# Second norm's column sums set one by one between large products, the hand-written order carried through the fourth pair, and other banks and scaling in the last norm

## The chip, the cores and the metric

One NeuronCore of a Trainium2 chip. The metric is the device time of one execution in microseconds (us); the time before is the median of 3 runs, and one further execution was profiled. Engines: PE is TensorE, DVE VectorE, ACT ScalarE, POOL GpSimd, SP SyncE (it issues the DMAs).

## The reference

One decoder layer on x of 1 x 1024 x 1024 in float32, with a final norm (D_MODEL 1024, D_FF 4096, 16 heads of 64, 2 key/value heads, window 128):

```python
def rms_norm(x, g):
    y = xf * lax.rsqrt(jnp.mean(xf * xf, axis=-1, keepdims=True) + RMS_EPS)
    return (y * g.astype(jnp.float32)).astype(x.dtype)

x = x + swa_mixer(rms_norm(x, attn_norm), w_qkv, sinks, w_o)   # sliding window 128, sinks, ALiBi
u = rms_norm(x, mlp_norm) @ w_up
x = x + square(relu(u)) @ w_down                               # 1024 -> 4096 -> 1024
out = rms_norm(x, final_norm)
```

The last lines are put together from the reference's layer; the change touches the second norm, the product with w_up, and the last norm.

## The kernel before

**Layout.** Features lie on the 128 partitions, tokens along the free axis, so h[0] to h[7] hold 128 features x 1024 tokens each. The tokens are cut into two halves (HALVES, 0 to 511 and 512 to 1023). A product in float32 is made of three passes over operands that are split in a high and a low part (names with _h and _l): high x high, high x low, low x high. So a "product of a 128x128 block" is three matmuls of 512 columns. A split is a copy on ScalarE (the high part) and a subtraction on VectorE (the low part).

**Order of work.** Attention comes first; then the second part of the output projection, blocks o_m_hf of 12 matmuls each (oblock, m = 0 to 7, first for half 0, then for half 1); oadd adds a block to h on VectorE, and square puts its square, made on ScalarE, into one of three parts: the running sum sq_0 (m = 0 to 5) and sq_6, sq_7 alone. The second norm of a half takes 4 column sums of each part (a matmul of 128x1 with ones; stat_sum), makes 1/rms from them (rstd, five small VectorE operations n_st and one on ScalarE), a diagonal matrix dg of it, and one matmul that spreads it over the partitions (stat_bcast, n2b). first_half makes x = h * gain * n2b for half 0, second_half for half 1.

**The up product** is made for 16 pairs p of 256 hidden units, each by seven products (numbers 1 to 7) of sums and differences of quarters instead of eight, 12 matmuls each. Weights: wa (for products 1, 2), and from the sums of raw weights s1, s2 (ws, products 5, 6), s3, s4 (wt, 7, 3), and wb (a22, product 4). Inputs: xb (products 1, 2), xt (5, 6), xu (7, 4), xc (3). PSUM tags X, Y and Z hold the sums of a pair; snapshot copies X to oa or ob, and relu2, c11_relu, c11_add and up_evac add, square and store the results.

**Who sets the order.** TensorE runs in the order of the code everywhere. VectorE, ScalarE and GpSimd do so while `e.ordered` is set: from the second half of the output projection through product (6, 2), where (n, p) is product n of pair p. After that a scheduler places their operations. The queue `tiny` holds single small matmuls: each call of mm takes one of them after its own matmul, as the first norm's sums do:

```python
    def mm(out, lhsT, rhs, start, stop, **kw):
        pe.matmul(out, lhsT=lhsT, rhs=rhs, start=start, stop=stop, **kw)
        if tiny:
            tiny.pop(0)()
```

**Slots.** Split weights of later pairs come from a ring of twelve slots over three tags (walloc, ring_up); raw weights wu come by DMA in two loads per pair (up_load, or up_first and up_sums), and four GpSimd operations make their sums sa and sb (in place for pair 2).

**The tail.** Seven down products of the same kind; the last (6) goes in four output blocks mp for each quarter of the tokens, ps_q[q][mp], of 256 columns; mmq issues their matmuls, and VectorE adds each finished block to h. finish is the last norm of a stretch of tokens: sums, diagonal, broadcast n3b, and eight multiplications with gain and n3b, two to an output DMA.

Line 41 of the profile is the helper that emits every operation, so groups are told apart by tile.

Of the kernel before, what the change touches and what calls it, by code (L numbers as in the profile page):

```python
# [62 lines left out]
def trunk(tc, xT, gains, wqkv, wo, wup, wdn, bias_d, sinks_d, ident_d, mask_d, outT):  # L63
# [588 lines left out]
    def square(m, hf):  # L652
# [17 lines left out]
    def his(src, alloc, name):  # L670
# [38 lines left out]
    def b22_split(i):  # L709
        XP["b22", i] = split1(h[2 * i + 1][:, HALVES[1]], atile if i else ktile, f"xc{i}")  # L710
# [153 lines left out]
    for p in range(2):  # L864
        WU["a22", p] = split1(SUM[p][0][:, 1], wtile, f"wb{p}")
# [4 lines left out]
    def oblock(m, hf):  # L870
        ps = bank(obanks[(hf * KT + m) % 5], f"o1_{m}_{hf}")
        for kk in range(4):
            mm3(ps, wsl(ws[m // 2], (m % 2) * 4 + kk), o_t[4 + kk], HALVES[hf], kk == 0, kk == 3)
# [11 lines left out]
    for m in range(KT):  # L885
        ps = oblock(m, 1)
# [6 lines left out]
        if m == 6:  # L893
            WU["s2", 0], WU["s1", 0] = LO["ws0"]()
        oadd(m, 1, ps)
        if m == 0:
            stat_sum(0)
# [14 lines left out]
    WU["s3", 0], WU["s4", 0] = LO["wt0"]()  # L912
    up_mms(1, 0, {2: lambda: stat_sum(1)})
    LO["wa3"] = his(wu3, ktile, "wa3")
# [7 lines left out]
    for p in range(4):  # L922
# [12 lines left out]
        if p == 1:  # L935
            LO["ws1"] = his(SUM[1][1], otile, "ws1")
        second_half(p + 1, rb)
        XP["t2", p], XP["t1", p] = LO[p]()
        up_mms(2, p + 1)
# [36 lines left out]
    c11_relu(0)  # L976
    up_product(6, 2)
    LO["wt1"] = his(SUM[1][2], otile, "wt1")
    WU["s3", 1], WU["s4", 1] = LO["wt1"]()
    c11_relu(1)  # L980
    c11_add(3)
    for e in (v, s, g):
        e.ordered = False
    for i in range(4):
        b22_split(i)
    for p in (2, 3):
        c11_relu(p)
    WU["a22", 2] = split1(u2[1][:, 1], walloc, "wb2")
    WU["s3", 2], WU["s4", 2] = split2(u2[0], walloc, "wt2")
# [198 lines left out]
```

## Time and profile before

| | |
|---|---|
| median of 3 runs | 942.75 us (941.77 to 943.16) |
| profiled execution, its own time | 944.29 us |
| its span | 942.4 us |
| mean granted clock of TensorE | 0.988 |
| PE busy | 918.4 us, 97% |
| DVE busy | 685.3 us, 73% |
| ACT busy | 445.9 us, 47% |
| POOL busy | 291.4 us, 31% |

The span is the time between the first and the last event on the chip; the execution's own time has 1.9 us beside it. The busy shares are means over all stages. A change in one stage is read in the rows of that stage: when an instruction starts, how long it takes, and, in brackets, how long its engine stood idle ahead of it and what ended that.

### The profile page before, as it was taken

What the parts mean: (1) busy time and instruction counts of PE and PEld (TensorE: products, weight loads), DVE (VectorE), ACT (ScalarE), POOL (GpSimd) and SP (SyncE); (2) the same over time, 40 slices, a digit from 0 to 9 for tenths busy, and PEclk for the clock granted to TensorE, in tenths of its full rate; (3) what the DMA queues carried; (4) which work ended last, traced back from release to release, by engine and by line L of the source; (5) the groups of instructions that cost most, each with busy time, mean ns of one, the idle gap of its engine ahead of it and who ended that gap; (6) DMA issues with size and microseconds to landing.
All of it is one profiled execution on the core that took longest, in us unless ns stands there. A gap on an engine that the chain in (4) does not pass through costs nothing.

```text
span 942.4 us, 12606 instructions
## 1 busy us (share of the span) xinstructions
PE 918.4 (97%) x4508; PEld 770.5 (82%) x4508; DVE 685.3 (73%) x956; ACT 445.9 (47%) x846; POOL 291.4 (31%) x254
## 2 busy tenths in 40 slices
PE   8999999999989998999999999999999999999996
PEld 6788888888878776888888888878888888888995
DVE  6789988989738886766675656566968785567964
ACT  8578877877524363433433343334333333445510
POOL 3026656566354015464435543110000000040200
PEclk9999999999989999999999999999999999999998
DMA  8200100510552124544354345789898988347622
GB/s 307 68 29 29 53 29 7 210 43 23 170 160 96 34 89 177 184 165 145 135 173 162 135 142 165 278 281 395 302 359 318 349 299 310 116 157 271 264 90 89
DMA packets 57325, 160.35 MB, mean 170 GB/s; under 512 B 6448, under 2 KB 10288, under 8 KB 57264
## 3 DMA queue, kind: packets, MB, share of 16 engines
q1 hardware_dynamic: 57264, 159.57, 47.7%
q8 instruction: 35, 0.57, 0.3%
q14 instruction: 26, 0.21, 0.1%
HBM read 121.79 MB, written 37.75 MB: 169 GB/s over the span
## 4 chain that ended last, share of the span: by engine, by line
PE 89%; DVE 4%; ACT 3%; issue 1%; POOL 1%; DMA 1%; SPq 0%; DVEq 0%; POOLq 0%; ACTq 0%
PE d L41 33%; PE uX L41 17%; PE f L41 12%; PE uY L41 9%; PE o L41 5%; PE uZ L41 4%; PE pv L41 3%; PE S L41 3%; PE pt L41 1%; PE psv L41 1%; PE psk L41 1%; DMA xr<-xT 1%; PE n2s L41 1%; ACT kh L41 1%; PE n L41 0%
## 5 line engine op out<-in xcount | busy, mean ns | idle before, releaser
L41 PE MATMUL d<-dx_h,dw_h 128*128 128x512 f32 (+1 forms) x512 | 186.5, 364 | 1.0 <-DVE hr L41 1.0
L41 PE MATMUL d<-dx_l,dw_h 128*128 128x512 f32 (+1 forms) x512 | 185.6, 362 | 0.0
L41 PE MATMUL d<-dx_h,dw_l 128*128 128x512 f32 (+1 forms) x512 | 185.6, 362 | 0.0
L41 PEld LDWEIGHTS d<-dx_h,dw_h 128*128 128x128 f32 x512 | 96.6, 189 | 16.8 <-DVE hr L41 1.4
L41 PEld LDWEIGHTS d<-dx_l,dw_h 128*128 128x128 f32 x512 | 96.6, 189 | 15.2 <-issue 0.2
L41 PEld LDWEIGHTS d<-dx_h,dw_l 128*128 128x128 f32 x512 | 96.6, 189 | 14.9
L41 ACT CAST dx_h<-hr 128x1024 fp32r<-128x1024 f32 x56 | 58.5, 1051 | 58.2 <-DVE dx_l L41 23.2
L41 ACT CAST dw_h<-wf 128x1024 fp32r<-128x1024 f32 x40 | 42.0, 1052 | 89.6 <-PE d L41 78.4
L41 DVE TENSOR_TENSOR dx_l<-hr,dx_h 128x1024 fp32r<-128x1024 f32 x56 | 71.6, 1287 | 17.4 <-ACT dx_h L41 16.4
L41 POOL TENSOR_TENSOR ssq3a<-ssq3a,sq_a 128x512 f32<-128x512 f32 x7 | 12.5, 1792 | 208.7 <-ACT sq_a L41 208.3
L41 DVE TENSOR_TENSOR dw_l<-wf,dw_h 128x1024 fp32r<-128x1024 f32 x40 | 48.7, 1220 | 26.0 <-ACT dw_h L41 25.9
L41 POOL TENSOR_TENSOR t<-t,sm 128x512 f32<-128x512 f32 x32 | 33.4, 1042 | 105.1 <-DVE sm L41 105.1
L41 DVE TENSOR_TENSOR wf<-wd,we 128x1024 f32<-128x1024 f32 x40 | 49.6, 1247 | 21.9 <-DMA we<-wdn 10.7
L41 ACT ACTIVATE t<-t,sm 128x129 f32<-128x129 f32 x128 | 50.5, 397 | 10.9 <-DVE sm L41 10.4
L41 PE MATMUL f<-xh,w_h 128*128 128x512 f32 x128 | 53.3, 416 | 0.0
L41 PE MATMUL f<-xl,w_h 128*128 128x512 f32 x128 | 50.4, 394 | 0.0
L41 PE MATMUL f<-xh,w_l 128*128 128x512 f32 x128 | 50.3, 393 | 0.0
L41 PE MATMUL uX<-xu_h,wb 128*128 128x512 f32 x128 | 43.4, 401 | 2.5 <-ACT oa L41 2.5
L41 POOL TENSOR_TENSOR ob<-ob,oa 128x512 f32<-128x512 f32 x16 | 21.6, 1348 | 78.3 <-DVE ob L41 78.3
L41 POOL TENSOR_TENSOR oc<-oc,oa 128x512 f32<-128x512 f32 x16 | 21.0, 1315 | 75.7 <-DVE oc L41 75.7
L41 ACT COPY oa<-uX 128x512 f32<-128x512 f32 x32 | 18.7, 588 | 49.9 <-PE uX L41 49.9
L41 POOL TENSOR_SCALAR_AFFINE_SELECT cur<-hl 128x1024 fp32r<-128x1024 f32 x32 | 39.5, 1235 | 2.0 <-DVE hl L41 2.0
(350 smaller groups left out, 2400.7 us busy)
## 6 DMA issues: line engine op xcount, KB each, us to landing
wd<-wdn SPq DMA_DIRECT2D x56, 512.0 KB, 5.8
hr<-hid SPq DMA_DIRECT2D x56, 512.0 KB, 5.0
we<-wdn SPq DMA_DIRECT2D x40, 512.0 KB, 6.8
hid<-oa SPq DMA_DIRECT2D x32, 256.0 KB, 2.4
hid<-oc SPq DMA_DIRECT2D x32, 256.0 KB, 2.2
hid<-ob SPq DMA_DIRECT2D x32, 256.0 KB, 2.3
w_r<-wqkv SPq DMA_DIRECT2D x8, 512.0 KB, 4.0
h<-xT SPq DMA_DIRECT2D x8, 512.0 KB, 6.4
```

The costliest lines, as they stand in the source:

```text
L41: ins = method(*args, **kw)
```

## The change

It has three parts. First, stat_part queues the second norm's sums in `tiny`, one between two large matmuls; for half 0 in o_0_1 (parts sq_6, sq_7, sq_0), for half 1 the running sum in the second half of o_7_1, sq_6 and sq_7 in product (1, 0). In half 1 the running sum's last addition goes to GpSimd, and some splits and one load move. Second, the hand-written order reaches through pair 3, with the products of pairs 0 to 3 in another order. Third, in the last product neighbouring blocks mp lie in different banks, and the last stretch's norm scales by the gain on ScalarE beforehand, so that three VectorE operations and two output DMAs remain.

```diff
+    def stat_part(hf, i):
+        first, last = (i == 1, i == 0) if hf == 0 else (i == 0, i == 2)
+        if first:
+            stat["ps", hf] = bank("Y", f"n2s{hf}")
+        ps, sq = stat["ps", hf], stat["sq", hf][i]
+        for b in range(4):
+            tiny.append(lambda b=b: pe.matmul(
+                ps[:, b:b + 1], lhsT=sq[:, b * P:(b + 1) * P], rhs=ones[:, 0:1], start=first and b == 0,
+                stop=last and b == 3, skip_group_check=True))
     def stat_sum(hf):
-        ps = bank("Y", f"n2s{hf}")
-        parts = stat.pop(("sq", hf))
-        for i, sq in enumerate(parts):
-            colsum(ps, sq, 4, i == 0, i == len(parts) - 1)
-        rn2 = rstd(ps, 4, f"n2_{hf}")
+        while tiny:
+            tiny.pop(0)()
+        rn2 = rstd(stat["ps", hf], 4, f"n2_{hf}")
...
-            (g if m < 5 else v).tensor_tensor(parts[0], parts[0], sq, op=ALU.add)
+            (v if hf == 0 and m == 5 else g).tensor_tensor(parts[0], parts[0], sq, op=ALU.add)
...
-        return ring(W * 2 + O * 2 + [ktile, atile] + W * 4 + O * 2)
+        return ring(W * 2 + O * 2 + [atile, atile] + W + O * 2 + W * 3)
...
-    for p in range(2):
-        WU["a22", p] = split1(SUM[p][0][:, 1], wtile, f"wb{p}")
...
     for m in range(KT):
-        ps = oblock(m, 1)
+        if m == 0:
+            for i in (1, 2, 0):
+                stat_part(0, i)
+        ps = oblock(m, 1, (lambda: stat_part(1, 0)) if m == 7 else None)
+        if m == 0:
+            stat_sum(0)
         if m == 1:
             rb = stat_bcast(0)
...
+        if m in (3, 4):
+            WU["a22", m - 3] = LO["wb", m - 3]()
         oadd(m, 1, ps)
         if m == 0:
-            stat_sum(0)
...
+        if m in (1, 2):
+            LO["wb", m - 1] = his1(SUM[m - 1][0][:, 1], wtile, f"wb{m - 1}")
...
     s2_2 = up_sums_inplace(2, *u2)
-    up_mms(1, 0, {2: lambda: stat_sum(1)})
+    stat_part(1, 1)
+    stat_part(1, 2)
...
+    up_mms(1, 0)
+    stat_sum(1)
...
     up_product(6, 2)
...
+    up_mms(7, 0)
+    c22_sum(0)
...
+    up_mms(7, 1)
+    c22_sum(1)
+    WU["s3", 2], WU["s4", 2] = LO["wt2"]()
+    s2_3 = up_sums_inplace(3, *u3)
+    up_product(4, 0)
+    up_product(3, 0)
+    d1_sum(1)
+    c11_relu(2)
+    up_product(4, 1)
+    up_mms(5, 2)
+    up_product(3, 1)
+    c11_relu(3)
+    WU["s2", 3] = split1(s2_3, walloc, "ws3a")
...
+    up_product(7, 2)
+    WU["s3", 3], WU["s4", 3] = split2(u3[0], walloc, "wt3")
+    up_product(6, 3)
+    up_product(4, 2)
+    EARLY = 4
+    raw4 = up_first(EARLY, walloc)
+    up_mms(5, 3)
+    up_product(3, 2)
+    up_sums(EARLY, raw4, temp)
+    up_product(7, 3)
     for e in (v, s, g):
         e.ordered = False
...
-    order = [(7, 0), (7, 1), (4, 0), (3, 0), (5, 2), (4, 1), (6, 3), (3, 1), (7, 2), (5, 3), (4, 2), (3, 2),
-             (7, 3), (1, 4), (4, 3), (2, 4), (3, 3)]
+    order = [(4, 3), (2, EARLY), (3, 3)]
...
+        if t1 == T:
+            rb = ps[:, 0:n].unsqueeze(1)
+            for i in range(2):
+                k, hg = 4 - i, hgs[i]
+                v.tensor_tensor(hg[:, 0:k], hg[:, 0:k], rb.to_broadcast([P, k, n]), op=ALU.mult)
+                if i:
+                    v.scalar_tensor_tensor(hg[:, k], h[7][:, sl], gn[:, 2, 7:8], ps[:, 0:n],
+                                           op0=ALU.mult, op1=ALU.mult)
+                nc.sync.dma_start(outT[:, 4 * i:4 * i + 4, sl], hg)
+            return
...
-    ps_q = [[banks[2 * q + mp // 2][:, (mp % 2) * 256:(mp % 2) * 256 + 256] for mp in range(4)] for q in range(2)]
+    ps_q = [[banks[2 * q + mp % 2][:, (mp // 2) * 256:(mp // 2) * 256 + 256] for mp in range(4)] for q in range(2)]
...
+            for m in (2 * mp, 2 * mp + 1) if mp < 2 else (4, 5, 6):
+                s.activation(hgs[m // 4][:, m % 4], h[m][:, 768:1024], AF.Copy, scale=gn[:, 2, m:m + 1])
```

TensorE, from the last block of the output projection's half 0 into block o_0_1 of half 1 (o is the block's PSUM bank, wo a weight, oh and ol the attention's output; n2s holds the column sums). Before:

```order
L41 MATMUL o_0_1_3142<-oh_2741,wo_0_l 128x512
L41 MATMUL n2s_3158<-ones,sq_0_0_3023 128x1 x4
L41 MATMUL n2s_3158<-ones,sq_6_0_3124 128x1 x4
L41 MATMUL n2s_3158<-ones,sq_7_0_3140 128x1 x4
L41 MATMUL o_1_1_3194<-oh_1876,wo_0_h 128x512
```

Now:

```order
L41 MATMUL o_0_1_3137<-oh_1876,wo_0_h 128x512
L41 MATMUL n2s_3136<-ones,sq_6_0_3118 128x1
L41 MATMUL o_0_1_3137<-ol_1877,wo_0_h 128x512
L41 MATMUL n2s_3136<-ones,sq_6_0_3118 128x1
L41 MATMUL o_0_1_3137<-oh_1876,wo_0_l 128x512
L41 MATMUL n2s_3136<-ones,sq_6_0_3118 128x1
```

The twelve sums stood in one block behind o_0_1; now each has a large matmul ahead of it, the first one behind the first matmul of o_0_1. In half 1 the running sum is asked for in o_7_1, now:

```order
L41 MATMUL o_7_1_3334<-oh_2473,wo_3_h 128x512
L41 MATMUL n2s_3341<-ones,sq_0_1_3172 128x1
L41 MATMUL o_7_1_3334<-ol_2474,wo_3_h 128x512
L41 MATMUL n2s_3341<-ones,sq_0_1_3172 128x1
L41 MATMUL o_7_1_3334<-oh_2473,wo_3_l 128x512
```

where before all twelve sums of half 1 stood behind the ninth matmul of product (1, 0).

VectorE, from the norm's small operations of half 0 (n_0_st) to the first x products (wb is the low part of a22 of pairs 0 and 1, dg the diagonal). Before:

```order
L41 TENSOR_TENSOR h_2044<-o_0_1_3142,h_2044 128x512
L41 TENSOR_SCALAR n_0_st<-n2s_3158 128x4
L41 RECIPROCAL n_0_st<-n_0_st 128x4
L41 TENSOR_TENSOR n_0_st<-n_0_st 128x4
L41 SCALAR_TENSOR_TENSOR n_0_st<-n_0_st 128x4
L41 TENSOR_TENSOR wb_3003<-wu0b,wb_3003 128x512
L41 TENSOR_TENSOR wb_3006<-wu1b,wb_3006 128x512
L41 SCALAR_TENSOR_TENSOR n_0_st<-n_0_st 128x4
L41 TENSOR_TENSOR dg_0_3178<-ident,n_0_st 128x512
L41 TENSOR_TENSOR h_2046<-o_1_1_3194,h_2046 128x512
L41 SCALAR_TENSOR_TENSOR x_0_3213<-h_2044,gn,n2b_3207 128x512
```

Now:

```order
L41 TENSOR_TENSOR h_2058<-o_7_0_3120,h_2058 128x512
L41 TENSOR_SCALAR n_0_st<-n2s_3136 128x4
L41 RECIPROCAL n_0_st<-n_0_st 128x4
L41 TENSOR_TENSOR n_0_st<-n_0_st 128x4
L41 SCALAR_TENSOR_TENSOR n_0_st<-n_0_st 128x4 x2
L41 TENSOR_TENSOR dg_0_3169<-ident,n_0_st 128x512
L41 TENSOR_TENSOR h_2044<-o_0_1_3137,h_2044 128x512
L41 TENSOR_TENSOR h_2046<-o_1_1_3184,h_2046 128x512
L41 SCALAR_TENSOR_TENSOR x_0_3203<-h_2044,gn,n2b_3197 128x512
```

The two wb splits no longer stand between the small operations and the diagonal; they stand later, behind the splits of x_1 and x_2. The add of o_0_1 stands behind the diagonal now.

ScalarE, around the copies of product 7 of pairs 0 and 1 (oa from uX; xc, wt, ws and wb are high parts). Before:

```order
L41 CAST wt_h<-wu2c 128x1024
L41 CAST xc_3663<-h_2058 128x512
L41 COPY oa_3400<-uX_3362 128x512
L41 COPY oa_3440<-uX_3427 128x512
L41 CAST ws_h<-sa_3702 128x1024
L41 CAST wb_3712<-wu3b 128x512
```

Now:

```order
L41 CAST xc_3655<-h_2050 128x512
L41 CAST xc_3664<-h_2054 128x512
L41 CAST xc_3666<-h_2058 128x512
L41 COPY oa_3396<-uX_3366 128x512
L41 ACTIVATE oa_3436<-oa_3436 128x512 x2
L41 CAST wt_h<-wu2c 128x1024
L41 COPY oa_3436<-uX_3423 128x512
L41 ACTIVATE oc_3730<-uX_3366 128x512
```

The copy of pair 0 stood behind the wt cast of pair 2, and the ws cast, which reads GpSimd's sums of pair 3, right behind the copies; now the wt cast follows the copy of pair 0, and the two relus of pair 1 stand between.

## Rows read from the trace of the kernel before

**Rows 1.** Page, part 1: busy us, share of the span, instructions.

```profile
PE 918.4 (97%) x4508; PEld 770.5 (82%) x4508; DVE 685.3 (73%) x956; ACT 445.9 (47%) x846; POOL 291.4 (31%) x254
```

**Rows 2.** Windows: busy of PE, PEld, DVE, ACT, POOL; granted clock; DMA share; GB/s.

```profile
260.00:280.00 20.00, 17.81 (x84) 14.67 (x82) 6.56 (x14) 5.85 (x9) 11.54 (x10) 0.91 0.43 140
274.00:276.00 2.00, 2.00 (x6) 1.51 (x6) 0.70 (x4) 0.00 (x0) 0.56 (x1) 0.50 0.20 33
```

**Rows 3.** TensorE's timeline, second norm: start, us, operation, count, [idle before <-releaser].

```profile
267.90 0.39 PE L41 MATMUL o<-oh,wo_h 128*128 128x512 f32 x1
...
270.62 2.73 PE L41 MATMUL n2s<-ones,sq 128*128 128x1 f32 x24
...
280.41 1.83 PE L41 MATMUL n2b<-dg,ones 128*128 128x512 f32 x2 [2.60 <-DVE dg L41]
281.25 1.41 PE L41 MATMUL o<-oh,wo_h 128*128 128x512 f32 x1
...
308.42 1.02 PE L41 MATMUL n2b<-dg,ones 128*128 128x512 f32 x2
```

**Rows 4.** TensorE's timeline, 346 to 377 us, from (7, 1) to (4, 2).

```profile
346.07 0.39 PE L41 MATMUL uX<-xu_h,wt_l 128*128 128x512 f32 x1
348.24 0.50 PE L41 MATMUL uX<-xu_h,wb 128*128 128x512 f32 x1 [1.77 <-ACT oa L41]
...
372.42 0.50 PE L41 MATMUL uY<-xt_h,ws_h 128*128 128x512 f32 x1 [2.13 <-DVE ob L41]
...
376.86 0.40 PE L41 MATMUL uX<-xu_h,wb 128*128 128x512 f32 x1
```

**Rows 5.** TensorE's timeline, first norm's sums between large matmuls.

```profile
30.27 0.28 PE L41 MATMUL n_ps<-ones,ssq 128*128 128x1 f32 x2
...
30.73 0.28 PE L41 MATMUL n_ps<-ones,ssq 128*128 128x1 f32 x2
```

**Rows 6.** Timelines of ACT, DVE and POOL, second norm, picked.

```profile
267.94 0.63 ACT L41 ACTIVATE sq<-h 128x512 f32<-128x512 f32 x1 [3.86 <-DVE h L41]
...
278.26 0.69 DVE L41 TENSOR_TENSOR wb<-wu0b,wb 128x512 fp32r<-128x512 f32 x1 [3.49 <-ACT wb L41]
...
279.67 0.69 DVE L41 TENSOR_TENSOR dg<-ident,n_st 128x512 f32<-128x512 f32 x1
...
282.28 2.72 DVE L41 SCALAR_TENSOR_TENSOR x<-h,gn,n2b 128x512 f32<-128x512 f32 x4 [1.32 <-PE n2b L41]
284.92 1.22 DVE L41 TENSOR_TENSOR xb_l<-x,xb_h 128x1024 fp32r<-128x1024 f32 x1
...
287.97 2.01 DVE L41 TENSOR_TENSOR xb_l<-x,xb_h 128x1024 fp32r<-128x1024 f32 x1
...
295.43 0.68 DVE L41 TENSOR_TENSOR h<-o,h 128x512 f32<-128x512 f32 x1
...
287.61 1.30 POOL L41 TENSOR_TENSOR sq<-sq,sq 128x512 f32<-128x512 f32 x1 [4.57 <-ACT sq L41]
```

**Rows 7.** ScalarE's timeline, copies and casts of the middle.

```profile
347.61 1.06 ACT L41 COPY oa<-uX 128x512 f32<-128x512 f32 x2
...
369.45 1.05 ACT L41 CAST ws_h<-sa 128x1024 fp32r<-128x1024 f32 x1 [6.02 <-POOL sa L41]
```

**Rows 8.** TensorE's timeline, last product, between two blocks.

```profile
911.45 0.28 PE L41 MATMUL d<-dx_h,dw_l 128*128 128x256 f32 x1
912.24 0.39 PE L41 MATMUL d<-dx_h,dw_h 128*128 128x256 f32 x1 [0.52 <-DVE hr L41]
```

**Rows 9.** VectorE's timeline at the end; window (VectorE's busy, clock, DMA share, GB/s).

```profile
935.88 3.22 DVE L41 SCALAR_TENSOR_TENSOR out<-hr,gn,n3b 128x256 f32<-128x256 f32 x8 [0.79 <-PE n3b L41]
...
940.00:940.50 0.50, 0.00 (x0) 0.50 0.98 340
```

**Rows 10.** Timelines of ACT and PE, pair 5: sums' cast, first use.

```profile
392.08 1.06 ACT L41 CAST ws_h<-sa 128x1024 fp32r<-128x1024 f32 x1
...
414.95 0.39 PE L41 MATMUL uX<-xt_h,ws_h 128*128 128x512 f32 x1
```

More of the change, by code (lines that the diff above doesn't have):

```diff
@@ L677, in los, with his1 @@
             return [(hi[:, i], lo[:, i]) for i in range(2)]
+        return los
+    def his1(src, alloc, name):
+        x = two(alloc(F32R, name))
+        s.copy(x[:, 0], src)
+        def los():
+            v.tensor_tensor(x[:, 1], src, x[:, 0].bitcast(F32), op=ALU.subtract)
+            return x[:, 0], x[:, 1]
         return los
@@ L911, in trunk @@
     s2_2 = up_sums_inplace(2, *u2)
-    WU["s3", 0], WU["s4", 0] = LO["wt0"]()
-    up_mms(1, 0, {2: lambda: stat_sum(1)})
-    LO["wa3"] = his(wu3, ktile, "wa3")
+    stat_part(1, 1)
+    stat_part(1, 2)
+    LO["wa3"] = his(wu3, wtile, "wa3")
+    WU["s2", 0], WU["s1", 0] = LO["ws0"]()
+    up_mms(1, 0)
+    stat_sum(1)
     snapshot(1, 0)
@@ L934, in trunk @@
         snapshot(1, p + 1)
-        if p == 1:
+        if p == 0:
+            LO["wt0"] = his(SUM[0][2], otile, "wt0")
+        if p == 2:
             LO["ws1"] = his(SUM[1][1], otile, "ws1")
@@ L938, in trunk @@
         XP["t2", p], XP["t1", p] = LO[p]()
+        if p == 0:
+            WU["s3", 0], WU["s4", 0] = LO["wt0"]()
         up_mms(2, p + 1)
@@ L976, in trunk, with c22_sum, d1_sum @@
     c11_relu(0)
-    up_product(6, 2)
-    LO["wt1"] = his(SUM[1][2], otile, "wt1")
-    WU["s3", 1], WU["s4", 1] = LO["wt1"]()
-    c11_relu(1)
-    c11_add(3)
+    LO["wt1"] = his(SUM[1][2], wtile, "wt1")
+    LO["wb", 2] = his1(u2[1][:, 1], walloc, "wb2")
+    b22_his(0)
+    WU["s3", 1], WU["s4", 1] = LO["wt1"]()
+    WU["a22", 2] = LO["wb", 2]()
+    up_product(6, 2)
+    b22_his(1)
+    b22_lo(0)
+    c11_add(3)
+    u3 = up_load(3)
+    b22_lo(1)
+    b22_his(2)
+    b22_his(3)
+    def c22_sum(p):
+        c22 = OUT["a", p][:, 1]
+        OUT["d", p] = temp(f"od{p}")
+        s.copy(c22, PS["X", p])
+        v.tensor_tensor(c22, PS["Y", p], c22, op=ALU.add)
+        relu2(c22, c22)
+        store(5, p, c22)
+    def d1_sum(p):
+        c11, c22 = OUT["a", p][:, 0], OUT["a", p][:, 1]
+        v.tensor_tensor(OUT["d", p][:, 0], c11, c22, op=ALU.add)
+        store(1, p, OUT["d", p][:, 0])
+    up_mms(7, 0)
+    c22_sum(0)
+    b22_lo(2)
+    b22_lo(3)
+    c11_relu(1)
+    LO["wt2"] = his(u2[0], walloc, "wt2")
+    d1_sum(0)
+    up_mms(7, 1)
[11 more added lines that the diff above has]
+    WU["s2", 3] = split1(s2_3, walloc, "ws3a")
+    WU["s1", 3] = split1(u3[1][:, 0], walloc, "ws3b")
+    WU["a22", 3] = split1(u3[1][:, 1], walloc, "wb3")
+    up_product(7, 2)
[8 more added lines that the diff above has]
+    up_product(7, 3)
     for e in (v, s, g):
         e.ordered = False
[L984 to L989, printed above, removed]
-    EARLY = 4
-    order = [(7, 0), (7, 1), (4, 0), (3, 0), (5, 2), (4, 1), (6, 3), (3, 1), (7, 2), (5, 3), (4, 2), (3, 2),
-             (7, 3), (1, 4), (4, 3), (2, 4), (3, 3)]
+    up_product(1, EARLY)
+    up_splits(EARLY)
+    order = [(4, 3), (2, EARLY), (3, 3)]
     for p in range(EARLY, NG):
@@ L996, in trunk @@
         order += ([(1, nxt)] if nxt < NG else []) + [(4, p)] + ([(2, nxt)] if nxt < NG else []) + [(3, p)]
-    ready = 3
     for n, p in order:
-        if (n, p) == (7, 1) or (n == 6 and p >= EARLY - 1):
-            while ready <= min(max(p + 1, 3), NG - 1):
-                raw = up_first(ready, walloc) if ready >= EARLY else None
-                up_sums(ready, raw, temp)
-                up_splits(ready)
-                ready += 1
+        if n == 6 and p + 1 < NG:
+            up_sums(p + 1, up_first(p + 1, walloc), temp)
+            up_splits(p + 1)
         up_product(n, p)
@@ L1112, in trunk @@
     fa = None
+    hgs = []
     for gg in range(NG // 2):
@@ L1117, in trunk @@
             for mp in range(4):
-                mmq(0, 2 * gg + e, mp, 2 * gg + e == 0 and mp % 2 == 0)
+                mmq(0, 2 * gg + e, mp, 2 * gg + e == 0 and mp < 2)
         if gg < 4:
@@ L1129, in trunk @@
         for g_ in range(NG):
-            mmq(1, g_, mp, g_ == 0 and mp % 2 == 0)
+            mmq(1, g_, mp, g_ == 0 and mp < 2)
             if g_ in (5, 11):
```

19 lines of the change are left out of this document (11 added, 8 removed).

## The prediction, made before the changed kernel was run

> **What bounds the kernel now.** I read the page's busy shares first. TensorE is busy 97% of the span [rows 1], so the time falls only where TensorE waits or runs slowly. The windows come next: the granted clock of the 20 us from 260 is 0.91, and inside it there is a stretch at 0.50, the lower of the two levels, 1.2 rather than 2.4 GHz [rows 2]. Last I read TensorE's timeline through the two places that the change rewrites, the second norm [rows 3] and the hand-over from the hand order to the later pairs [rows 4].
>
> The pace comes from rows 3: twelve large products start between 267.90 and 270.62, 2.72 us, so one takes 0.227 us. The price of one fall of the clock comes from rows 4: after the wait at 372.42, twelve products take until 376.86, 4.44 us, so a fall costs 4.44 − 2.72 = 1.72 us. What went ahead of a fall is in the same rows: the 24 one-column products from 270.62, and idle stretches of 2.60, 1.77 and 2.13 us [rows 3, 4].
>
> **The second norm.** From 267.90 to the second half's broadcast at 308.42, TensorE takes 40.52 us [rows 3]. What it has to do there: 117 large products (12 for each of o_0_1 to o_7_1, 12 of product 1, 9 of product 2), 117 × 0.227 = 26.5; 24 column sums of two passes, 2 × 2.73 = 5.5; one broadcast of two passes, about two large products, 0.45. That is 32.4, and 8.1 are lost: the 2.60 idle, and the rest the slow clock behind the sums and behind the idle.
>
> The change sums the same columns, one between two large products. The first norm does this already: from one sum there to the next is 0.46 us [rows 5], of which 0.227 is the large product, so a spread sum costs 0.23, and 24 cost 5.6. So the spreading by itself saves no TensorE work (0.1 more). It can win only what is lost now, 8.0 at most.
>
> What of it comes back, in order. (1) The first single sum needs sq_6, which ScalarE has at 267.94 + 0.63 = 268.57 [rows 6], while TensorE now wants it after one large product, at 267.90 + 0.23 = 268.13: a new wait of 0.4, with the hand-over 0.5. (2) The sums then end at 268.4 + 5.5 = 273.9, o_1_1 at 276.6. The chain to the diagonal stood behind the two weight splits wb in VectorE's order, which waited 3.49 us [rows 6]; with them gone from there it has 2.7 us of o_1_1 as cover, and its own length is the five small operations and the 0.69 of the diagonal, about 2. So I take no wait here; the broadcast starts at 276.6 and o_2_1 at 277.1, not 281.25. (3) VectorE's x products start when the broadcast has ended (1.02 at full clock [rows 3]), at 277.65 rather than 282.28. From there to the add of o_5_1 at 295.43 VectorE had 13.15 us of work without a gap [rows 6]; the two wb splits now stand in between, 2 × 0.65 more. So that add comes at 292.1, then 0.68 for it, 0.63 for the square on ScalarE, 1.30 for GpSimd's add, which the change has put in VectorE's place, and 0.2 of hand-overs: the running sum is ready at 294.9. (4) TensorE asks for it after the seventh matmul of o_7_1, at 277.1 + 5 × 2.72 + 7 × 0.227 = 292.3. It waits 2.6 there; before, nothing was asked for until o_7_1 and three quarters of product 1 were through. Behind that sum on TensorE's queue stand the rest of o_7_1 and all of product 1, so nothing fills the wait.
>
> How sure is 2.6? One split of x took 2.01 us at 287.97 and its neighbour 1.22, with GpSimd's add from 287.61 for 1.30 beside the long one [rows 6]. Two of the four are long; if the shifted times keep both apart from GpSimd, the wait shrinks by 2 × 0.79 to about 1.1; if the other two are hit as well, it grows to 4.2. I take 2.6, where the order of VectorE and GpSimd against each other stays as it is. The Trainium skill (SBUF — State Buffer, Who interferes with whom) says that a VectorE instruction with two SBUF inputs contends with a GpSimd instruction that reads SBUF, and that the first to issue holds the shared ports for its whole length. The trace agrees as far as it goes: 0.94 of GpSimd's add was left when the long split began, and the split took 0.79 longer. By that rule the add moved to GpSimd would also meet the split of x_3, which makes the wait the upper bound of 4.2, another 1.6 from the gain (the third rival below).
>
> (5) After an idle stretch of 2.6 the clock fell before [rows 3], so I take one fall, 1.72. Gain of this part: 8.0 − 0.5 − 2.6 − 1.7 = **3.2**.
>
> The other moved steps here (loads of u2, splits of wt0, wa3 and ws1) lie on engines with room, and their users are products 3 to 7 and pair 3, tens of microseconds later; I take zero. Without that cover a 1024-wide split is 1.22.
>
> **The middle.** From 346.30 (0.23 behind the last product at 346.07) to 376.86 eight up products of 12 stand on TensorE: 8 × 2.72 = 21.76 of 30.56 us, 8.8 lost [rows 4]: two named waits of 1.77 and 2.13, two falls of 3.44 together, and small waits and restarts. The first wait is for the copy of uX(7,0), which ScalarE began only at 347.61, behind casts and relus; the second is for ob, whose copy stood on ScalarE behind the cast of sa for pair 4, and that cast waited 6.02 us for GpSimd's sums [rows 7]. The hand order removes both causes: the copy of uX(7,0) stands behind three short casts and can start when (7,0) ends, 2.72 ahead of the 346.30 at which (4,0) needs it; the casts of pair 4's sums now stand behind the last copy of pair 3. What could be late next is the low part of ws3a, which (6,3) asks for in its third product: some twenty VectorE operations stand ahead of it in the new order, and I can fix its cover to no better than half a microsecond; I keep 0.3 as lost. Gain: **8.5**; bounds 4.7 (one wait of 2.13 with its fall stays, 3.85) and 8.8.
>
> **The tail.** Twice in the last product TensorE waits for VectorE to empty the bank that it writes next: 911.45 to 912.24 is 0.79, and a product of 256 columns is half of 0.227, so 0.68 is lost [rows 8], and the same at the end of the third block. With neighbouring blocks in different banks both go: 1.4. The last scaling: now the eight operations take 3.22, so the first output leaves after two, 0.8 [rows 9]. The new first multiply is 128x1024 from PSUM, not in the trace; the nearest row is the 128x512 add from PSUM, 0.68 [rows 6], so 1.2 to 1.36, and the first output leaves 0.4 to 0.55 later. The DMA engines are full (0.98) until shortly before the end [rows 9], so I let the end follow the first output, −0.5; if it followed VectorE's last operation, it would gain 0.5. Gain: **0.9** (0.7 to 1.8).
>
> **Sum.** 3.2 + 8.5 + 0.9 = 12.6. The profiled execution took 944.29, 1.54 above the median; 944.29 − 12.6 − 1.54 = 930.15, so **930.2**.
>
> **Rivals.**
> - The running sum is in time. Speaks for it: the contended splits may fall otherwise, and the bound goes down to 1.1, shorter than each of the three waits in the rows that a fall followed. Against: VectorE's chain has no gap. Then 8.0 − 0.5 comes back, a total of 16.9: **925.9**.
> - The spreading does not do what it says: the clock falls behind the first spread as it fell behind the block (or, at nearly the same price, the wait for the running sum is the 4.2 above). For: the share of one-column passes in it is the largest of the kernel, 5.5 us of alternation; against: the large products keep coming. Another 1.7 lost: **931.9**.
> - The middle keeps one wait: ScalarE's and VectorE's hand order there is full, and a single late load of pair 3 stops all behind it. 2.13 + 1.72: **934.0**.
> - Slower: the later pairs. The ring of weight slots is re-dealt, and the sums of pairs 5 to 15 on GpSimd stand in this loop. Now the cast for pair 5 begins at 392.08 and TensorE uses it at 414.95 [rows 10], a cover of 22.9 us less the cast. Were it used up, each of 11 pairs would wait; from 12.6 / 11 = 1.15 us each the kernel is slower than before. **943 or more**; the cover speaks against it.
>
> **How the numbers follow.** Forecast 0.40, sum in time 0.20, fall in the first spread 0.20, a wait in the middle 0.13, slower or level 0.07. The predicted time is the first one's. The range 925.0 to 936.0 takes in the first four with the bounds of the tail, and of the longer wait. A measurement here tells about 0.2%, 1.9 us, from no change. All four cases are faster by more than that: 0.93; the rest is split 0.03 same and 0.04 slower.
>
> **What the changed profile would show.** Right: a wait of TensorE of 0.5 for sq_6 near 268, no idle at the first broadcast, o_2_1 near 277, one wait of 1 to 4 us in o_7_1 for the running sum with GpSimd as releaser and a stretch at 0.50 behind it; TensorE without idle from 346 to 377; no bank waits in the tail. Wrong: a clock of 0.50 right behind the first spread, a wait at the diagonal, idle at (6,3) or in pair 4, or waits that recur once a pair behind 400.

## The result, and the profile after

The changed kernel takes 933.61 us (median of 10 executions, 932.67 to 939.80) against 942.64 for the kernel before (10 executions, 941.77 to 943.91): 0.9926 of it, 95% interval 0.9903 to 0.9950, so 9.0 us faster by the medians. The forecast was 930.2, the range 925.0 to 936.0.

The ten executions fall in two groups: six take 932.7 to 933.7 us at a mean granted clock of TensorE of 0.995 to 0.997 (the lower group from here on), four 938.1 to 939.8 at 0.988 to 0.990 (the upper group). The profiled one, 939.76, is of the upper group; what follows is read with that in mind. Its page begins:

```profile
span 938.0 us, 12589 instructions
PE 916.8 (98%) x4508; PEld 771.0 (82%) x4508; DVE 685.5 (73%) x951; ACT 446.7 (48%) x854; POOL 290.6 (31%) x255
```

To see where the time went I cut both timelines at five matmuls that stand in every kernel of this study: the first matmul of o_0_1, the second of (6, 0), the first of (6, 5), the first of (4, 15), behind the only wait that those pairs have, the last large matmul. The lengths in us, differences of start times in TensorE's timeline (the last one up to the span):

| stretch | before | changed | gain |
|---|---|---|---|
| second norm, products 1 and 2: o_0_1 to (6, 0) | 58.65 | 60.52 | −1.87 |
| middle: (6, 0) to (6, 5) | 88.40 | 83.16 | 5.24 |
| later pairs: (6, 5) to (4, 15) | 199.39 | 199.39 | 0.00 |
| (4, 15) and on, down products | 317.23 | 315.69 | 1.54 |
| end: last large matmul to the span's end | 10.83 | 11.72 | −0.89 |

With 0.38 ahead of o_0_1 these make up the 4.4 us between the two profiled spans; the 9.0 are by the medians. So the later pairs gave nothing back, the middle is the gain, and the second norm, in this execution, lost. Its rows, TensorE's timeline of the changed kernel (they answer to [rows 3]):

```profile
267.52 0.39 PE L41 MATMUL o<-oh,wo_h 128*128 128x512 f32 x1
268.48 0.38 PE L41 MATMUL n2s<-ones,sq 128*128 128x1 f32 x2 [0.58 <-ACT sq L41]
...
276.57 1.02 PE L41 MATMUL n2b<-dg,ones 128*128 128x512 f32 x2
277.03 0.79 PE L41 MATMUL o<-oh,wo_h 128*128 128x512 f32 x1
...
294.79 0.38 PE L41 MATMUL n2s<-ones,sq 128*128 128x1 f32 x2 [2.00 <-POOL sq L41]
...
304.62 0.42 PE L41 MATMUL n2s<-ones,sq 128*128 128x1 f32 x2
...
309.93 1.02 PE L41 MATMUL n2b<-dg,ones 128*128 128x512 f32 x2
```

The first four rows stand where the forecast put them: a wait of 0.58 for sq_6, no wait at the first broadcast, o_2_1 at 277.03. The wait for the running sum is 2.00, forecast at 2.6. What was not forecast is the length of what follows. Windows of TensorE in the changed kernel (busy, granted clock, DMA share, GB/s):

```profile
296.00:308.00 12.00, 12.00 (x39) 0.50 0.06 23
310.00:312.00 2.00, 2.00 (x9) 1.00 0.42 168
```

In these twelve microseconds, and by windows of 1 us from about 295.5 to 309.1, so for 13.6 us, the granted clock is 0.50, while TensorE counts as busy all the time. From 294.79 to 309.93 stand 12 single sums and 26 large matmuls: at full clock 12 × 0.233 + 26 × 0.227 = 8.7, here 15.1, so 6.4 us are lost, not 1.7. That is also the distance between the medians of the two groups, 933.2 and 939.5; no trace of another of the ten executions is kept, so that the other three of the upper group lost their time here too is not shown. VectorE, ScalarE and GpSimd ahead of the wait:

```profile
277.63 2.73 DVE L41 SCALAR_TENSOR_TENSOR x<-h,gn,n2b 128x512 f32<-128x512 f32 x4 [0.17 <-PE n2b L41]
...
290.80 1.21 DVE L41 TENSOR_TENSOR xb_l<-x,xb_h 128x1024 fp32r<-128x1024 f32 x1
291.93 1.27 DVE L41 TENSOR_TENSOR h<-o,h 128x512 f32<-128x512 f32 x2
...
292.70 0.63 ACT L41 ACTIVATE sq<-h 128x512 f32<-128x512 f32 x1 [1.10 <-DVE h L41]
...
293.47 1.27 POOL L41 TENSOR_TENSOR sq<-sq,sq 128x512 f32<-128x512 f32 x1 [0.32 <-ACT sq L41]
```

The chain is the one of the forecast: x at 277.63, the add of o_5_1 at 291.93 (forecast 292.1), square, GpSimd's last addition, ready at 294.74 (forecast 294.9). The split of x_3 at 290.80 took 1.21: it ended at 292.01, and GpSimd's last addition began at 293.47.

The middle, TensorE's timeline (answers to [rows 4]):

```profile
355.67 0.39 PE L41 MATMUL uX<-xu_h,wb 128*128 128x512 f32 x1
357.70 0.50 PE L41 MATMUL uY<-xt_h,ws_l 128*128 128x512 f32 x1 [1.64 <-DVE ob L41]
...
395.71 0.39 PE L41 MATMUL uY<-xt_h,ws_l 128*128 128x512 f32 x1
397.47 0.50 PE L41 MATMUL uX<-xu_h,wt_h 128*128 128x512 f32 x1 [1.37 <-ACT ob L41]
```

Both waits of before are gone and two others stand here, 1.64 at the first matmul of (5, 2) and 1.37 at the first of (7, 4). VectorE and GpSimd ahead of the first:

```profile
348.79 3.48 DVE L41 TENSOR_TENSOR xc<-h,xc 128x512 fp32r<-128x512 f32 x2
352.19 1.78 DVE L41 TENSOR_TENSOR od<-oa 128x512 f32<-128x512 f32 x1
...
356.96 0.68 DVE L41 TENSOR_TENSOR ob<-uY,ob 128x512 f32<-128x512 f32 x1
...
348.40 1.62 POOL L41 TENSOR_TENSOR s<-wu3b,wu3c 128x512 f32<-128x512 f32 x1
349.98 1.74 POOL L41 TENSOR_TENSOR wu3b<-wu3b 128x512 f32<-128x512 f32 x1
351.67 1.76 POOL L41 TENSOR_TENSOR wu3c<-wu3c,s 128x512 f32<-128x512 f32 x1
```

While GpSimd made the sums of pair 3, two splits xc took 1.74 each and the sum od 1.78; alone, such an operation takes 0.69. ob of (3, 0), which frees the bank of (5, 2), came at 356.96. ScalarE and GpSimd ahead of the second:

```profile
394.42 1.05 ACT L41 CAST ws_h<-sa 128x1024 fp32r<-128x1024 f32 x1 [4.22 <-POOL sa L41]
396.84 0.57 ACT L41 COPY ob<-uX 128x512 f32<-128x512 f32 x1
...
379.32 1.29 POOL L41 TENSOR_TENSOR ob<-ob,oa 128x512 f32<-128x512 f32 x1 [3.87 <-DVE ob L41]
380.57 1.30 POOL L41 TENSOR_TENSOR sb<-wu4a,wu4b 128x512 f32<-128x512 f32 x1
...
389.43 2.02 POOL L41 TENSOR_TENSOR sb<-wu5a,wu5b 128x512 f32<-128x512 f32 x1 [2.91 <-DMA wu5b<-wup]
```

It is the wait of [rows 7] one pair later: the copy ob stands on ScalarE behind three casts, the first of which waits for GpSimd's sums, now those of pair 5. Last the tail. TensorE's two waits behind the last product before (beside [rows 9]):

```profile
932.87 0.61 PE L41 MATMUL n<-ones,sq_last 128*128 128x1 f32 x4 [0.23 <-ACT sq_last L41]
935.14 0.70 PE L41 MATMUL n3b<-dg,ones 128*128 128x256 f32 x2 [1.67 <-DVE dg L41]
```

TensorE and VectorE in the changed kernel (answers to [rows 8, 9]):

```profile
926.28 0.28 PE L41 MATMUL d<-dx_h,dw_l 128*128 128x256 f32 x1
...
927.88 0.61 PE L41 MATMUL n<-ones,sq_last 128*128 128x1 f32 x4 [0.53 <-ACT sq_last L41]
930.15 1.08 PE L41 MATMUL n3b<-dg,ones 128*128 128x256 f32 x2 [1.67 <-DVE dg L41]
...
931.27 2.09 DVE L41 TENSOR_TENSOR hg<-hg,n3b 128x1024 f32<-128x1024 f32 x2 [1.17 <-PE n3b L41]
933.27 0.47 DVE L41 SCALAR_TENSOR_TENSOR hg<-hr,gn,n3b 128x256 f32<-128x256 f32 x1
```

No wait for a bank is left in the last product. The end takes 0.89 longer, in three places: TensorE waits 0.30 longer for the last square; the broadcast n3b, at a granted clock of 0.59 in its 1.08 us (1.00 before), takes 0.38 longer; and from the start of the first multiplication to the end of the span pass 6.73 us, 0.21 more than the 6.52 before.

### The profile page after: what moved, and what is told of

Read it like the earlier page. It is cut to its first block, busy times and chain, and to the rows that moved or that the text cites. A ratio compares the mean times of both kernels' runs of the same rounds, so it can differ in the third digit from the quotient of the medians.

```text
span 938.0 us, 12589 instructions
## 1 busy us (share of the span) xinstructions
PE 916.8 (98%) x4508; PEld 771.0 (82%) x4508; DVE 685.5 (73%) x951; ACT 446.7 (48%) x854; POOL 290.6 (31%) x255
## 4 chain that ended last, share of the span: by engine, by line
PE 82%; DVE 8%; ACT 3%; issue 3%; POOL 2%; DMA 1%; SPq 0%; DVEq 0%; POOLq 0%; ACTq 0%
PE d L41 33%; PE uX L41 16%; PE f L41 12%; PE uY L41 7%; PE uZ L41 4%; PE pv L41 3%; PE S L41 3%; PE pt L41 1%; PE o L41 1%; DVE x L41 1%; POOL sb L41 1%; POOL sa L41 1%; PE psv L41 1%; PE psk L41 1%; DVE xb_l L41 1%
```

## The experiments

Each kernel is the one named with the edit shown. The kernel before was run beside them. Where a stretch is given, it is cut as in the table above.

### Half 1's sums later

```diff
-        ps = oblock(m, 1, (lambda: stat_part(1, 0)) if m == 7 else None)
+        ps = oblock(m, 1, None)
...
+    stat_part(1, 0)
     stat_part(1, 1)
     stat_part(1, 2)
```

> The changed kernel, but in half 1 the four column sums of the running sum sq_0 also go into product (1, 0), ahead of those of sq_6 and sq_7, and no longer into o_7_1. Theory A (the wait of 2.0 us for GpSimd's last addition is what the clock falls behind, and the 13.6 us at 0.50 in the profiled execution, 6.8 us lost, are the whole difference between the two groups of times of the changed kernel, 932.7 to 933.7 and 938.1 to 939.8): no wait at the running sum, no stretch at 0.50 near 295, one group of times near 931. Rival B (the spread sums alone make the clock fall, wait or not): the wait goes, the stretch at 0.50 stays in some executions, and two groups remain, near 931 and 937. Rival C (the diagonal's chain, which now ends closer to the broadcast, takes the wait over): a wait of 0.5 us or more at the second broadcast, 932.5 or more.

Six executions: 931.67 to 933.54 and one of 938.89 (clock 0.989); median 932.88. The profiled one, 932.34, shows a wait of 0.66 for the running sum, no stretch at 0.50 in it, and a first stretch of 52.97. So a wait was left, and one execution lies where the upper group is: neither A nor B came out clean. No broadcast waited (against C).

### The same wait, sums in blocks behind it

```diff
             if late and kk == 2:
                 late()
+                while tiny:
+                    tiny.pop(0)()
...
-    stat_part(1, 1)
-    stat_part(1, 2)
...
     up_mms(1, 0)
+    stat_part(1, 1)
+    stat_part(1, 2)
     stat_sum(1)
```

> The changed kernel, with the running sum asked for at the same place in o_7_1, but its four column sums in one block there, and the eight others in one block behind product (1, 0); nothing is spread behind the wait. Theory A2 (the wait lets the clock fall, and the small products between the large ones keep it down): a stretch at 0.50 behind the wait of at most about 3.5 us, as behind the idle stretches of before, so no execution above 936; all within 932.5 to 935.5. Rival (the long stretch belongs to the wait, whatever follows it): two groups as in the changed kernel, one near 939.

Five executions, 934.75 to 937.18, median 935.20; none at 939. TensorE's wait and the window behind it:

```profile
294.73 1.05 PE L41 MATMUL n2s<-ones,sq 128*128 128x1 f32 x8 [2.23 <-POOL sq L41]
...
296.00:299.00 3.00, 3.00 (x8) 0.50 0.00 0
300.00:302.00 2.00, 2.00 (x14) 1.00 0.33 131
```

The wait is as long (2.23), the clock falls as before, and it is back at 1.00 by 300. So a fall came behind the wait without any spreading behind it, and what differs from the changed kernel is the single sums between the large matmuls there; with them the clock stayed down four times as long (13.6 and 3.4 us). All five lie above the changed kernel's lower group, so that group seems to go without a fall; this is argued from the times alone. Two executions, 935.77 and 937.18, lay above the bounds that I gave.

### The spreading undone

```diff
-        if m == 0:
-            for i in (1, 2, 0):
-                stat_part(0, i)
-        ps = oblock(m, 1, (lambda: stat_part(1, 0)) if m == 7 else None)
+        ps = oblock(m, 1)
         if m == 0:
+            for i in (1, 2, 0):
+                stat_part(0, i)
             stat_sum(0)
...
-    up_mms(1, 0)
-    stat_sum(1)
+    up_mms(1, 0, {2: lambda: ([stat_part(1, i) for i in range(3)], stat_sum(1))})
```

> The changed kernel with the spreading alone undone: the twelve sums of half 0 in a block behind o_0_1, those of half 1 in a block behind the ninth product of (1, 0), as before; the moved splits, the addition on GpSimd and the rest stay. Theory A: the waits of 0.6 and 2.0 go (gain 2.6), each block is followed by one stretch at 0.50 as in the kernel before (2 x 1.72 lost), none of 13.6 us: one group, near 934. Rival B (spreading is worth more: the falls of before behind the blocks cost what the forecast put on them, 8.0 together): 938 or more, since the idle at the diagonal comes back too.

Four executions, 932.00 to 933.23, median 932.61, one group: no slower than the changed kernel's lower group, and without the upper one. Of the 24 executions of this kernel and of those below that are built on it none lies more than 3 us above the lowest of its kernel. TensorE and its windows:

```profile
269.86 2.73 PE L41 MATMUL n2s<-ones,sq 128*128 128x1 f32 x24
275.32 1.02 PE L41 MATMUL n2b<-dg,ones 128*128 128x512 f32 x2
...
294.55 2.73 PE L41 MATMUL n2s<-ones,sq 128*128 128x1 f32 x24
300.64 1.12 PE L41 MATMUL n2b<-dg,ones 128*128 128x512 f32 x2 [0.47 <-DVE dg L41]
...
273.00:277.00 4.00, 4.00 (x17) 1.00 0.45 114
297.00:301.00 4.00, 3.53 (x16) 1.00 0.00 0
```

The blocks of 24 one-column passes are back, and behind neither does the clock fall in this execution; the first stretch takes 51.73. In the kernels below that are built on this one, the profiled executions show one or two falls there and 52.6 to 54.2. So a block is not always followed by a fall, and the spreading as it stands gains nothing. The one fall from 262 to 411 us in this execution stands behind the wait of 1.83 at (5, 2); the middle takes 84.99.

### The kernel before with the wb splits moved

```diff
...
-    for p in range(2):
-        WU["a22", p] = split1(SUM[p][0][:, 1], wtile, f"wb{p}")
...
+        if m in (3, 4):
+            WU["a22", m - 3] = LO["wb", m - 3]()
         oadd(m, 1, ps)
...
+        if m in (1, 2):
+            LO["wb", m - 1] = his1(SUM[m - 1][0][:, 1], wtile, f"wb{m - 1}")
```

> The kernel before, with one thing changed: the splits wb of pairs 0 and 1 stand where the changed kernel has them, behind the splits of x_1 and x_2, and not between the norm's small operations and the diagonal. Theory F (of the second norm's gain nearly all comes from that move, not from the spreading): the wait of 2.60 us for the diagonal goes, and the stretch at 0.50 behind it, 2.60 + 1.72, so about 938.5. Rival G (the chain is still late, since sums in a block end the same and clock falls behind them): the wait shrinks below 1 us but TensorE loses it again at the blocks, 940.5 or more.

```profile
270.45 2.73 PE L41 MATMUL n2s<-ones,sq 128*128 128x1 f32 x24
275.91 1.02 PE L41 MATMUL n2b<-dg,ones 128*128 128x512 f32 x2
```

The broadcast stands without idle (2.60 before), and the first stretch takes 53.52, 5.1 less than before. The profiled execution, 939.05, is by as much faster than that of before. The median is not: 940.80 (12 executions, 938.47 to 943.16), a ratio of 0.9982, 0.9971 to 0.9994. The middle takes as long as before (88.48), with longer waits (1.77, 1.55 and 3.13) and one fall in place of two. From 262 to 411 us the profiled execution of before has five falls, this one two. By the mean clocks executions of one kernel differ in this: of the 17 executions of the kernel before that were run beside this one, ten had 0.991 or 0.992 and took 941.6 to 942.4 us, while the profiled one, 944.29 at 0.988, is one of the longest. So F names the place rightly, and the time is G's: 1.5 us by the medians, not 4.3. What else gives the second norm of the changed kernel its gain in the lower group is not shown.

### Pair 3's GpSimd sums left out

```diff
-    s2_3 = up_sums_inplace(3, *u3)
+    s2_3 = u3[1][:, 1]
```

> The changed kernel without GpSimd's four operations that make the sums of pair 3's weights; the raw weights are used in their place (this part of the computation is left out). Theory D (GpSimd's sums, now at the same time as VectorE's splits xc and the sum od, make three VectorE operations of 0.69 take about 1.75, 3.2 us in all, so ob of (3, 0) is late and (5, 2) waits 1.64): the three take about 0.7 each, no wait at (5, 2), 1.7 us faster than the changed kernel in the same group of its times, 931.5. Rival E (VectorE's order itself is too full there, the wt split ahead of ob): the wait stays above 1 us, 933.0.

VectorE's timeline of this kernel, the operations that were long:

```profile
346.53 1.29 DVE L41 TENSOR_TENSOR xc<-h,xc 128x512 fp32r<-128x512 f32 x2
347.74 0.69 DVE L41 TENSOR_TENSOR od<-oa 128x512 f32<-128x512 f32 x1
...
352.00 0.69 DVE L41 TENSOR_TENSOR ob<-uY,ob 128x512 f32<-128x512 f32 x1 [0.52 <-PE uY L41]
```

The two splits take 1.29 together, od 0.69, and the wait at (5, 2) is gone; the middle takes 81.26, 1.9 less. D holds, E falls. The time is not the expected one, 936.26 (five executions, 935.05 to 937.46): the profiled one has a stretch at 0.50 of some ten microseconds behind the wait of 1.96 for half 1's sum, and the others' clocks (0.988 to 0.991) are like it. The stretch begins at 297.2, behind the first four single sums, and ends at 307.4, behind the last one at 303.44; in the changed kernel too it ended, at 309.1, only behind the last one at 304.62. Why all five have it, I did not find out.

### Pair 3's sums later, on the kernel with the spreading undone

```diff
-    s2_3 = up_sums_inplace(3, *u3)
     up_product(4, 0)
+    s2_3 = up_sums_inplace(3, *u3)
```

> The kernel with the spreading undone, and GpSimd's sums of pair 3 issued behind product (4, 0) and its addition oc, not ahead of it. Theory D: VectorE's splits xc and the sum od take 0.7 each again, the wait of 1.83 us at (5, 2) goes or falls below 0.3, and if ws3a is still in time for (6, 3) the kernel takes 930.8. Rival J (the sums are then late for ws3a, which (6, 3) needs): the wait moves to (6, 3) with 1 us or more, 932 or more.

```profile
358.62 0.74 PE L41 MATMUL uX<-xt_h,ws3a 128*128 128x512 f32 x2 [0.82 <-DVE ws3a L41]
```

931.40 (930.35 to 932.29, four executions): the wait at (5, 2) is gone, and 0.82 of it is back at (6, 3) for ws3a, between D and J. The three VectorE operations take 0.64 and 0.68 here; od and oc of the next pair, now beside GpSimd, take 1.78. The contention went to operations that could wait.

### Pair 4's sums earlier, on the kernel with the spreading undone

```diff
     up_mms(5, 3)
+    up_sums(EARLY, raw4, temp)
     up_product(3, 2)
-    up_sums(EARLY, raw4, temp)
```

> The kernel with the spreading undone (932.6, one group), and GpSimd's sums of pair 4 issued ahead of product (3, 2) and no longer behind it. Theory H (the wait of 1.36 us at (7, 4) for the copy ob comes from GpSimd: the sums of pair 4 stand behind its last operation of (3, 2), idle 3.9 us ahead of that, so the raw weights of pair 4 are given up late, those of pair 5 land late, and ScalarE's copy of uX(6, 4) stands behind the cast of pair 5's sums): the wait goes, 1.4 to 1.7 faster, 931.0. Rival I (ScalarE's order decides: the cast of pair 5's sums stays ahead of the copy and waits for something else): the wait stays near 1.4, 932.6.

ScalarE and TensorE:

```profile
376.50 1.03 ACT L41 CAST wa_h<-wu5a 128x1024 fp32r<-128x1024 f32 x1
377.44 1.06 ACT L41 COPY oa<-uX 128x512 f32<-128x512 f32 x2
...
378.06 0.50 PE L41 MATMUL uX<-xu_h,wb 128*128 128x512 f32 x1 [1.63 <-ACT oa L41]
```

The wait at (7, 4) goes, and one of 1.63 stands at (4, 3) instead: with the sums there earlier, the scheduler put three casts ahead of the copies of (7, 3) and (1, 4). 932.93 (931.19 to 933.24), no gain. H was right about the cause at (7, 4) and wrong about the time.

### The last norm's scaling as before, on the kernel with the spreading undone

```diff
-        if t1 == T:
+        if False:
...
-            if mp % 2 == 0:
-                hgs.append(...)
-            for m in ...:
-                s.activation(hgs[m // 4][:, m % 4], h[m][:, 768:1024], AF.Copy, scale=gn[:, 2, m:m + 1])
```

> The kernel with the spreading undone, and the last norm's scaling as before (eight multiplications, four outputs of 256 KB, no scaled copies on ScalarE). Theory K (the new scaling lets the first output start later, and the end follows it; from the last large product to the end it took 10.8 us before and 11.7 after): 0.5 to 0.9 faster, 931.9. Rival L (the difference is the lower clock of the last broadcast, not the scaling): within 0.2 of 932.6.

931.68 (931.17 to 933.13), 0.9 less than 932.61, but the two sets overlap. In the profiled executions the end takes 10.90, against 11.35 with the new scaling: 0.45, just below K's 0.5. Only 0.16 of it is K's mechanism, the time from the first multiplication to the end (6.58 and 6.74); the other 0.29 is the longer wait for the last square (0.24 and 0.53), and the broadcast takes 0.70 in both, so L is not tested here. Over all profiled kernels the first of these times is 6.5 to 6.6 with the old scaling and 6.7 to 6.8 with the new one. The wait for the square is 0.53 in seven of nine kernels with the new scaling, and 0.23 or 0.24 in the other two and in all five with the old one; why, no run shows. Over all kernels run here the end took 10.8 to 11.4 with the old scaling and 11.0 to 11.9 with the new one.

### Spread sums without a long wait

```diff
-        first, last = (i == 1, i == 0) if hf == 0 else (i == 0, i == 2)
+        first, last = (i == 1, i == 0) if hf == 0 else (i == 1, i == 2)
...
-        ps = oblock(m, 1, (lambda: stat_part(1, 0)) if m == 7 else None)
+        ps = oblock(m, 1, None)
...
     stat_part(1, 1)
+    stat_part(1, 0)
     stat_part(1, 2)
```

> The changed kernel, all twelve sums of half 1 spread in product (1, 0), those of sq_6 first, the running sum's second, those of sq_7 last, so that the running sum is asked for 2 us later than with the sums in the order before. Theory B (spread sums alone let the clock fall in some executions and then hold it down): no wait at the running sum, and still some executions near 938 beside a group near 932. Theory A (it takes a wait of half a microsecond or more ahead of them): one group, 931 to 933.

931.95 to 932.58, four executions. The wait did not go but changed: 0.67 for sq_6 (ScalarE), so this kernel has a wait as long as that with half 1's sums later, from another cause. One group, with the clock at 1.00 in every window from 262 to 411 us; behind the wait:

```profile
295.16 0.38 PE L41 MATMUL n2s<-ones,sq 128*128 128x1 f32 x2 [0.67 <-ACT sq L41]
...
294.00:300.00 6.00, 5.33 (x36) 1.00 0.42 158
```

A kernel in which no square should be waited for, the sums in product (2, 0):

```diff
-        ps = oblock(m, 1, (lambda: stat_part(1, 0)) if m == 7 else None)
+        ps = oblock(m, 1, None)
...
-    stat_part(1, 1)
-    stat_part(1, 2)
...
-    stat_sum(1)
...
-    up_mms(2, 0, {2: lambda: bc.append(stat_bcast(1))})
+    for i in range(3):
+        stat_part(1, i)
+    up_mms(2, 0)
+    stat_sum(1)
+    up_mms(1, 1, {2: lambda: bc.append(stat_bcast(1))})
...
```

> The changed kernel, all twelve sums of half 1 spread in product (2, 0) and the broadcast in (1, 1), so late that TensorE can't wait for any of the squares. Theory B (twelve sums one by one between large products let the clock fall by themselves): executions with a stretch at 0.50 behind those sums, and a second group some 6 us above the fastest. Theory A (the fall needs a wait ahead of the sums; the sums only hold it down): no such stretch, one group within 2 us, near 931.5 if VectorE's later work on half 1 is still in time.

932.90 to 934.31, four executions, median 933.91, no wait at the sums and no stretch at 0.50 there; VectorE's later work costs a wait of 1.41 at (2, 1). Both kernels show one group, as A has it, but with eight executions in all: at one in six, as in the kernel with half 1's sums later, eight would show none about one time in four. The 938.89 there decides nothing between A and B: its kernel's profiled execution waits 0.66, which A allows, and no trace of that one is kept. Put together, with a wait of about 2 us ahead of single sums (the changed kernel, the one without pair 3's sums) nine of fifteen executions have a clock of 0.988 to 0.991. With a wait of 0.7 or less, or none (these two kernels and the one with half 1's sums later), one of fourteen has. That is on A's side, by counting and not by traces.

### Everything mended

To the kernel with the spreading undone come the three edits above (pair 3's sums later, pair 4's earlier, the old scaling), and

```diff
     up_mms(5, 2)
+    WU["s2", 3] = split1(s2_3, walloc, "ws3a")
     up_product(3, 1)
     c11_relu(3)
-    WU["s2", 3] = split1(s2_3, walloc, "ws3a")
...
+    up_product(1, EARLY)
+    up_splits(EARLY)
+    for n, p in ((4, 3), (2, EARLY), (3, 3), (6, EARLY)):
+        up_product(n, p)
     for e in (v, s, g):
         e.ordered = False
...
```

> The kernel with the spreading undone, and besides: GpSimd's sums of pair 3 behind product (4, 0), with the split ws3a ahead of the sums of (3, 1) on VectorE; the sums of pair 4 ahead of (3, 2), with the hand order kept through (6, 4), so that the copies stand ahead of the casts of the next pair's sums; the last norm's scaling as before. If the causes found so far are the right ones, the waits at (5, 2), (6, 3) and (7, 4) go (1.8 + 1.4 to 1.6, none of the 0.8), and the end comes 0.9 earlier: 932.6 - 1.9 - 1.5 - 0.9, about 928.5. If each wait only moves to the next place where ScalarE's or VectorE's order is tight, as in the kernel with pair 4's sums early, 930.5 or more.

929.48 (928.68 to 929.79, four executions), a ratio of 0.9856, 0.9841 to 0.9870: 4 us below the changed kernel, 13 below the one before. That is halfway between the two expectations. The waits at (5, 2), (6, 3) and (7, 4) are gone and the middle takes 80.80; one wait stands a few products on, in (4, 4), again for a copy that stands on ScalarE behind casts that wait for GpSimd's sums:

```profile
392.62 0.50 PE L41 MATMUL uX<-xu_h,wb 128*128 128x512 f32 x1 [0.95 <-ACT oa L41]
```

The same kernel was run again:

> The kernel with everything mended once more, for the size of its gain: four executions lay between 928.7 and 929.8. If its times are one group, again 928.7 to 930; if a long stretch at 0.50 can occur in it too, some near 936.

928.95 (928.27 to 931.20, four executions), ratio 0.9855, 0.9839 to 0.9872; one lies above 930, none near 936.

## Why the prediction came out as it did

The time lay in the range and the sign was right, but 9.0 us came where 12.6 were forecast. That it lies in the range is in part luck: four of the ten executions lie above 936.0, and with six of them there the median would have too.

**The sum.** Its last line takes off 12.6, read from the losses of the profiled execution, and then the 1.54 by which that execution lies above the median. By its clock (0.988, where most executions of that kernel have 0.989 to 0.991) and its five falls the 1.54 is probably a part of the same losses, taken off twice; without it the sum gives 931.7. This is argued: no other execution of the kernel before has a trace.

**Second norm, forecast gain 3.2.** Steps (1) to (4) held to 0.6 us or better: 0.58 for 0.5, o_2_1 at 277.03 for 277.1, the sum ready at 294.74 for 294.9, a wait of 2.00 for 2.6. Two of the splits of x were long again (1.97 and 1.95), as assumed. Step (5), "I take one fall, 1.72", failed in its size both ways. Its price was read behind a wait that only large matmuls followed [rows 4]; here single sums followed, and the stretch lost 6.4 in the profiled execution, which turned the part into −1.9. If the loss is not there in the lower group, 60.52 − 6.4 = 54.1, a gain of 4.5; the kernel with half 1's sums later, which has no fall there, shows 52.97. And the 8.1 lost before were read from an execution with more falls than most of that kernel have, by their mean clocks. The claim about what the spreading is worth failed too, though no term rested on it: with the sums in blocks and all else as changed, the time is the same or better. In the profiled executions what was gained came with the wb splits leaving the diagonal's chain, as step (2) has it; by the medians that move alone gave 1.5.

**The middle, forecast 8.5, measured 5.2.** "The hand order removes both causes" was right for the causes, and none of the two waits is left. I looked for what is late next on VectorE at (6, 3) alone. I did not ask what GpSimd's sums of pair 3 meet at their new place; that is the 1.64 at (5, 2), shown by leaving the sums out and by moving them. And I let the casts of pair 4's sums go behind pair 3's copies without asking which copy the casts of pair 5 now stand ahead of: 1.37 at (7, 4). Neither wait was followed by a fall in the profiled execution; with the spreading undone the one at (5, 2) was, and the middle took 84.99. So of the rivals, "the middle keeps one wait" came true in its mechanism, and its 934.0 is nearest to the median, by luck: it is the sum of other parts.

The Trainium skill (SBUF — State Buffer, Who interferes with whom) was weighed at the wrong place. For the split of x_3 it would have given a longer wait; the trace shows 1.21 there and no overlap with the addition moved to GpSimd. The price was wrong as well: one more split at the 0.79 of the rows makes the wait 3.4, and 4.2 takes two. In the middle the trace agrees with the same rule: two splits with both inputs in SBUF take 3.48 beside GpSimd's sums and 1.29 without them.

**The tail, forecast 0.9.** The bank waits gave 1.54 for 1.4. The scaling cost 0.45 between two kernels that differ in it alone, for 0.5, but mostly not as forecast: "I let the end follow the first output" gave 0.16 there and 0.21 here, although the first output was issued 0.38 later behind the first multiplication (1.28 and 0.90), as forecast; the rest is the later square, which the forecast did not have. In the profiled execution the end lost 0.89, with 0.38 of it from the broadcast's clock, so the tail gained 0.65 in all.

**The later pairs**, the slower rival: 199.39 in both kernels.

**What stays open.** Why the clock falls behind the wait of 2.0 in four executions of ten and not in the others; whether a wait of 0.66 is enough; why all five executions without pair 3's sums show it; what besides the wb splits helps the second norm; and why the last square comes 0.3 later.

## What to carry to other kernels

When a hand order moves work on GpSimd, look which VectorE operations with two inputs in SBUF will run beside it, and put it beside those that can wait. A wait that a cast ahead of a copy causes moved on each time that it was mended at one place: 2.13 at (5, 3) before, 1.37 at (7, 4) in the changed kernel, 0.95 at (4, 4) with everything mended. A small matmul put between large ones was cheap here (0.23) in nearly all executions in which TensorE waited 0.7 us or less ahead of it, and with a wait of 2 us nine executions of fifteen have the lower mean clock that a long stretch at 0.50 leaves: bring its operand early or leave it in a block, and time such a change over many executions. A loss that is read from one profiled execution belongs to that execution: before it is taken off the median, see whether that execution is a typical one.

## What the runs showed of the hardware that was not expected

- At a granted clock of 0.50 behind a wait of 2.00, twelve one-column sums between large matmuls went with a stretch of 13.6 us at the lower level; with the sums in two blocks behind a wait of 2.23 the stretch was under 4 us.
- Behind a block of 24 one-column passes the clock fell in both places of the kernel before and in neither in the kernel with the spreading undone.
- Beside GpSimd's additions of 512 columns, VectorE's 512-column operations with two inputs in SBUF took 1.74 to 1.78 and not 0.69; GpSimd's own took 1.62 to 1.76, against 1.3 alone.
